# Moving operands of the feed-forwards and of retention's sums at other bytes of a 256-byte line, each group at its own

## The chip, the cores and the metric

The kernel runs on one core of one Trainium2 chip. The metric is the device time in microseconds (us) of one execution; lower is better. Engines are named as in the profile: PE is TensorE's matmul side and PEld its weight load, DVE is VectorE, ACT is ScalarE, POOL is GpSimd, SP is SyncE, which issues most transfers.

## What is computed

Two layers over 512 latent tokens and 256 context tokens of width 1024. Layer 0 is windowed attention, layer 1 is bidirectional retention; each is followed by a SwiGLU feed-forward of width 2816, with the stream modulated ahead of each part. Cut to what matters here:

```python
def swiglu(h, w_in, w_out):
    gate, up = jnp.split(h @ w_in, 2, axis=-1)
    return (jax.nn.silu(gate) * up) @ w_out

def reference(x, c, ctx, c_ctx, ...):
    for i in range(DEPTH):
        ...
        h_x = modulate(rms_norm(x, norm1_g[i]), mx[0], mx[1])
        out_c, out_x = windowed_gqa_sink(...) if i == 0 else bidir_retention(...)
        x = x + mx[2] * out_x
        x = x + mx[5] * swiglu(modulate(rms_norm(x, norm2_g[i]), mx[3], mx[4]), ffn_w_in[i], ffn_w_out[i])
        if need_ctx_out:      # layer 0 alone: the context stream goes the same way
            ...
    return x

def bidir_retention(h_x, h_c, w_qkvg, ...):
    q_x, k_x, v_x, g_x = jnp.split(h_x @ w_qkvg, [qk, 2 * qk, 2 * qk + RET_VWIDTH], axis=-1)
    ...
```

## The kernel before

Activations lie transposed, 128 features on the partitions and tokens along the row, as eight tiles (k = 0 to 7) for 1024 features. Each fp32 value is kept as two parts, a high one (the value rounded to fp32r) and a low one (the rest), and each product is three matmuls: high weights x high activations, low x high, high x low (`mm3`, lines 148 to 150; `product`, line 994; `product_q`, 1413; `product_v`, 1426). ACT rounds (a cast), DVE subtracts (`split`, lines 165 and 166). Weights come as 128x1024 chunks (`wraw`, `wx`), are split into `whi` and `wlo` and used as stationary operand, 128x128 at a time; only `product_v` has the activations as stationary operand and 512 columns of weights moving.

Most large products are done by a seven-product scheme (`seven`): two halves of the inner dimension by two halves of the tokens, seven products instead of eight, with sums of activations (`token_sums`) and of weights (`quarter_sums`) made ahead. The operands are named "11", "12", "22" (the activations themselves) and 1 to 4 (their sums).

- Feed-forward 0 (about 392 to 872 us) has latent and context tokens in one row of 768, cut in two pieces of 384. `A[k, 0]` are tiles of the pool `ep`, tag `aq`; `A[k, 1]` and the sums `S` are tiles of `hq`, also tag `aq` (the helper `quarter`). All are moving operands of `product`. The same tag serves as a weight buffer in the last output group. While it runs, POOL issues 48 transfers of `adaw` (line 271), one behind the other, and DVE turns each into a column of layer 1's modulation (line 274).
- Retention (about 872 to 1368 us) has `h_sum`, the sums of the activations, in pool `hS`, tag `sA`: moving operands of `product_q` with 256 columns, stationary ones of `product_v`.
- Feed-forward 1 (about 1368 to 1716 us) has the activations `hx` (pool `hX`) and their sums `sA` (pool `fp`), 256 columns at a time, and the products' results `ax` (pool `fa`; a high and a low tile each), 512 columns, moving operands of the output products. Weights go round a ring of three pools, `rp`, `hW` and `fp`, two buffers each.

Pools are taken in order from the two ends of a partition, and in a pool the tags lie one behind the other in the order of their first tile. A tile of 512 or 768 fp32 columns is 8 or 12 times 256 bytes, so all tiles of a tag begin at the same byte of a 256-byte line. The helper `off_grid` puts a small tile into a pool (POOL writes zeros to it), by which what follows in the pool begins at another byte. A framework orders each engine's instructions and sets the semaphores from the tiles' uses; the time at which a tile's memory comes free is that of the last use of what lay there.

Of the kernel before, what the change touches and what calls it, by code (L numbers as in the profile page):

```python
# [9 lines left out]
F32R = mybir.dt.float32r  # L10
# [6 lines left out]
KT = D // P  # L17
# [32 lines left out]
def dit_kernel(ctx, tc, xT, cT, crow, small, consts, masks, tabs0, tabs1, jtab, adaQ, adaN, adaT, wst, out):  # L50
    nc = tc.nc
# [10 lines left out]
    def T(pool, cols, tag, bufs, dt=F32):  # L62
        return pool.tile([P, cols], dt, tag=tag, bufs=bufs, name=tag)
# [159 lines left out]
    def t_h(s):  # L223
        return T(hpool[0], 512, ("h", "hc")[s], (16, 8)[s], F32R)

    def off_grid(pool, cols):

        nc.gpsimd.memset(T(pool, cols, "off%d" % cols, 1), 0.0)

    def h_tiles(s):  # L230
        hi = t_h(s)
# [309 lines left out]
    with tc.manual_schedule(engines={mybir.EngineType.PE, mybir.EngineType.DVE, mybir.EngineType.Activation}):  # L541
# [56 lines left out]
        end = ada_unit(UNITS[0], wu[0])  # L598
# [11 lines left out]
        end = ada_unit(UNITS[1], wu[1])  # L610
# [320 lines left out]
    end = lambda: ends.pop(0)()  # L931
# [43 lines left out]
    ep = E.enter_context(tc.tile_pool(name="ep", bufs=1, reuse_waits="tile"))  # L975
# [4 lines left out]
    for s, d in WO_ORDER:  # L980
        out_part(s, d, 0, KT)
        if (s, d) == (1, 4):
            ln_exp_turn()
            scaled = rms(0, bank=pT)[1]
    A.close()

# [24 lines left out]
    hq = Q.enter_context(tc.tile_pool(name="hq", bufs=1, reuse_waits="tile", side="right"))  # L1011
    fp = F.enter_context(tc.tile_pool(name="fp", bufs=1, reuse_waits="tile"))
# [2 lines left out]
    bank = lambda n: T(psF, 512, n, 2)[:, 0:384]  # L1015
    fp32 = [T(ep, 2 * WIDE, "act", 5) for _ in range(4)]
    tm = [fp32[k % 4][:, k // 4 * WIDE:(k // 4 + 1) * WIDE] for k in range(KT)]
    A = {(k, 0): parts(T(ep, 768, "aq", 8, F32R)) for k in range(KT)}
    A.update({(k, 1): parts(quarter()) for k in range(KT)})

    def latent_shape(w):

# [53 lines left out]
    def new_act():  # L1076
        return T(ep, 2 * WIDE, "act", 5, F32R)
# [209 lines left out]
    for gsz in FFN_GROUPS:  # L1287
        acts = []
        for i in range(gsz):
# [4 lines left out]
            else:  # L1294
                a, end = seven(last_sum if f == PLAIN else None)
# [29 lines left out]
    hS = H.enter_context(tc.tile_pool(name="hS", bufs=1, reuse_waits="tile", side="right"))  # L1325
# [2 lines left out]
    qa = R.enter_context(tc.tile_pool(name="qa", bufs=1, reuse_waits="tile"))  # L1328
    qp = R.enter_context(tc.tile_pool(name="qp", bufs=1, reuse_waits="tile"))
    W4 = lambda n: T(psR, 512, n, 2)  # L1330
    h_sum = [(T(hS, 512, "sA", 16, F32R), T(hS, 512, "sA", 16, F32R)) for _ in range(KT)]
    h_first = [T(hpool[0], 512, "aq", 12, F32R) for _ in range(4)]
    h_rest = [(T(hpool[0], 512, "aq", 12, F32R), T(hpool[0], 512, "aq", 12, F32R)) for _ in range(4)]
    chunk_base = wpos[0]
# [160 lines left out]
    for hd in range(RH):  # L1495
# [187 lines left out]
        r, z = mv[:, 8:12], mv[:, 12:16]  # L1683
# [77 lines left out]
        if hd < RH - 1:  # L1761
            for d in range(KT):
# [4 lines left out]
        hM, hW, hX = (ctx.enter_context(tc.tile_pool(name=n, bufs=1, reuse_waits="tile", side="right"))  # L1767
                      for n in ("hM", "hW", "hX"))
        ahead = []

        def first_weights(room, behind=(), low=()):
            raw = w_raw()
            hi, lo = room()
            ahead.append((hi, lo))
            after(nc.scalar.copy(hi, raw), behind)
            after(nc.vector.tensor_tensor(lo, raw, hi, op=sub), low)

        wx_parts = lambda: (T(qw, 1024, "wx", 4, F32R), T(qw, 1024, "wx", 4, F32R))
        hW_parts = lambda: (T(hW, 1024, "whi", 2, F32R), T(hW, 1024, "wlo", 2, F32R))
        hm = [T(hM, 512, "hm", 8) for _ in range(KT)]  # L1780
        off_grid(hX, 16)
        hx = [(T(hX, 512, "hx", 16, F32R), T(hX, 512, "hx", 16, F32R)) for _ in range(KT)]
        off_grid(hX, 48)
        done = []

        def second_norm(k, c, behind=()):
# [17 lines left out]
                    after(ins, done[d - 4:d - 3])  # L1804
        done += [second_norm(k, HALVES[1]) for k in (KT - 2, KT - 1)]
        for i in (6, 7):
            first_weights(hW_parts, done[5:6], done[i:i + 1])

    scaled = []

# [10 lines left out]
    fa = F.enter_context(tc.tile_pool(name="fa", bufs=1, reuse_waits="tile"))  # L1821
    fp = F.enter_context(tc.tile_pool(name="fp", bufs=1, reuse_waits="tile"))
    ring += [rp, rp, hW, hW, fp, fp]
    wsel[0] = 4
    sh2 = T(fp, 16, "sh2", 1)
    sA = [(T(fp, 512, "sA", 16, F32R), T(fp, 512, "sA", 16, F32R)) for _ in range(KT)]
    off_grid(fp, 48)
    operand_a = operands(lambda k, half: [a[:, HALVES[half]] for a in hx[k]], sA)

    def new_act():  # L1830
        return T(fa, 512, "ax", 10, F32R), T(fa, 512, "ax", 10, F32R)

    def half(i):
        return [(a[:, HALVES[i]], b[:, HALVES[i]]) for a, b in hx]
# [245 lines left out]
```

## Time and profile before

| | |
|---|---|
| median of 3 runs | 1717.99 us (1717.43 to 1718.41) |
| profiled execution, first to last instruction | 1716.5 us (the profile has no other time of it) |
| PE busy | 1701.4 us, 11094 matmuls |
| DVE, ACT, POOL busy | 1337.5, 839.8, 124.2 us |
| granted TensorE clock | 1.000 |

The first number in a row of the order of time is the start in us from the span's start, the second the time until the last of its matmuls ended. A matmul's own time holds its way through the array, which overlaps the next one's; how fast PE goes is read from start to start. An `xN` joins N matmuls of the same names that follow each other. PE busy is therefore near 100% wherever it does not wait.

### The profile page before, as it was taken

The page shows a single profiled execution, that of the slowest core. Times are in us where ns is not written, and L with a number is a line of the kernel's source. Part 1 is how long each engine was busy: PE and PEld are TensorE (multiplying, and loading weights), DVE is VectorE, ACT ScalarE, POOL GpSimd, SP SyncE. Part 2 cuts the span into 40 slices and gives each one's busy share as a digit, 9 for nine tenths or more (in the row PEclk, how much of TensorE's full clock was granted, in tenths as well). Part 3 has the DMA queues.
Part 4 walks back from the last instruction along what each step waited for, and adds up shares of the span by engine and source line. Part 5 has one row for each costly group of instructions (what it writes and reads, how often), then busy time and mean ns, then how long its engine had stood idle before and what let it go on. Part 6 is the DMA issues. An engine that isn't in the chain of part 4 may idle for free.

```text
span 1716.5 us, 28196 instructions
## 1 busy us (share of the span) xinstructions
PE 1701.4 (99%) x11094; PEld 1535.9 (89%) x11094; DVE 1337.5 (78%) x2425; ACT 839.8 (49%) x1509; POOL 124.2 (7%) x266
## 2 busy tenths in 40 slices
PE   8999999999999999999999999999999999999999
PEld 5888878899999999999998898898898999999997
DVE  6897786488878787878799858758768998878774
ACT  5677786264424243343565624525434655445442
POOL 0033443000000000000000000000000100000000
PEclk9999999999999999999999999999999999999999
DMA  9500014233344434343434534433433333233322
GB/s 377 228 27 26 14 52 172 74 124 111 99 134 136 135 118 152 123 141 115 137 100 135 187 102 133 160 99 125 159 99 110 99 99 123 77 121 107 103 74 86
DMA packets 61908, 205.67 MB, mean 120 GB/s; under 512 B 6864, under 2 KB 7760, under 8 KB 61648
## 3 DMA queue, kind: packets, MB, share of 16 engines
q1 hardware_dynamic: 54864, 178.71, 31.2%
q0 software_dynamic: 6912, 25.17, 4.9%
q8 instruction: 87, 1.43, 0.3%
q14 instruction: 45, 0.37, 0.1%
HBM read 201.75 MB, written 2.10 MB: 119 GB/s over the span
## 4 chain that ended last, share of the span: by engine, by line
PE 87%; DVE 7%; DMA 3%; ACT 1%; issue 1%; POOL 0%; SPq 0%; DVEq 0%; ACTq 0%; POOLq 0%
PE Y L994 15%; PE Z L994 7%; PE pj L148 7%; PE pj L150 7%; PE pj L149 7%; PE Z L1426 6%; PE X L994 4%; PE Y L1413 3%; PE pO L809 2%; PE pT L784 2%; PE S L764 2%; PE pj L1426 2%; PE X L1413 2%; PE X L150 1%; PE Y L149 1%; PE Y L148 1%
## 5 line engine op out<-in xcount | busy, mean ns | idle before, releaser
L994 PE MATMUL Y<-aq,whi 128*128 128x384 f32 x640 | 173.4, 335 | 0.0
L254 DVE SCALAR_TENSOR_TENSOR res<-pj,mod,res 128x512 f32<-128x512 f32 (+1 forms) x102 | 74.3, 729 | 57.9 <-PE pj L150 57.3
L994 PEld LDWEIGHTS Y<-aq,whi 128*128 128x128 f32 x640 | 116.6, 188 | 0.7 <-DVE aq L1063 0.3
L140 ACT CAST whi<-wraw 128x1024 fp32r<-128x1024 f32 x75 | 78.4, 1050 | 68.0 <-PE Z L150 27.5
L141 DVE TENSOR_TENSOR wlo<-wraw,whi 128x1024 fp32r<-128x1024 f32 x75 | 91.2, 1222 | 20.4 <-ACT whi L140 19.7
L994 PE MATMUL Y<-aq,wlo 128*128 128x384 f32 x320 | 106.9, 334 | 0.0
L274 DVE CUSTOM_DVE_ANT_0 y<-adaw,crow,small_sb 128x1024 bf16<-128x1024 f32 x64 | 81.8, 1278 | 20.7 <-DMA adaw<-in_adaT_dram 20.7
L1343 ACT CAST whi<-wraw 128x1024 fp32r<-128x1024 f32 x55 | 57.4, 1050 | 69.9 <-PE Y L150 52.6
L1426 PE MATMUL Z<-whi,sA 128*128 128x512 f32 x256 | 80.4, 390 | 0.0
L1344 DVE TENSOR_TENSOR wlo<-wraw,whi 128x1024 fp32r<-128x1024 f32 x55 | 66.7, 1220 | 16.4 <-ACT whi L1343 16.3
L101 ACT ACTIVATE pr<-pr,stat,qs 128x513 f32<-128x513 f32 (+2 forms) x96 | 74.1, 775 | 10.0 <-DVE stat L771 7.2
L778 POOL TENSOR_SCALAR pr<-pr,stat 128x512 f32<-128x512 f32 (+2 forms) x96 | 67.3, 707 | 72.1 <-DVE stat L777 51.6
L148 PE MATMUL pj<-ax,whi 128*128 128x512 f32 x176 | 68.9, 392 | 0.0
L150 PE MATMUL pj<-ax,whi 128*128 128x512 f32 x176 | 68.7, 390 | 0.0
L149 PE MATMUL pj<-ax,wlo 128*128 128x512 f32 x176 | 68.5, 389 | 0.0
L271 POOL DMA_DIRECT2D adaw<-in_adaT_dram x48 | 25.6, 533 | 511.2 <-DVE mod L274 412.3
L148 PE MATMUL pj<-act,whi 128*128 128x512 f32 (+1 forms) x156 | 60.2, 386 | 0.5 <-DVE res L254 0.5
L994 PEld LDWEIGHTS Y<-aq,wlo 128*128 128x128 f32 x320 | 60.1, 188 | 0.0
L994 PE MATMUL Y<-sA,whi 128*128 128x256 f32 x304 | 60.0, 280 | 0.0
L149 PE MATMUL pj<-act,wlo 128*128 128x512 f32 (+1 forms) x156 | 60.0, 384 | 0.0
L150 PE MATMUL pj<-act,whi 128*128 128x512 f32 (+1 forms) x156 | 59.5, 382 | 0.0
L765 DVE CUSTOM_DVE_ANT_0 pr<-S,mask,qs 128x256 f32<-128x256 f32 (+1 forms) x96 | 52.8, 563 | 8.1 <-PE S L764 6.2
(626 smaller groups left out, 5574.8 us busy)
## 6 DMA issues: line engine op xcount, KB each, us to landing
wraw<-in_wst_dram SPq DMA_DIRECT2D x231, 512.0 KB, 3.7
adaw<-in_adaT_dram POOLq DMA_DIRECT2D x48, 512.0 KB, 3.9
wx<-in_wst_dram SPq DMA_DIRECT2D x28, 512.0 KB, 4.4
adan<-in_adaQ_dram SPq DMA_DIRECT2D x16, 512.0 KB, 6.7
adan<-in_adaN_dram SPq DMA_DIRECT2D x16, 512.0 KB, 8.3
res<-in_xT_dram SPq DMA_DIRECT2D x16, 256.0 KB, 5.1
q<-in_adaN_dram SPq DMA_DIRECT2D x16, 256.0 KB, 5.0
aq<-in_adaN_dram SPq DMA_DIRECT2D x12, 256.0 KB, 5.5
```

Of the source, the lines that this page charges most:

```text
L101: ins = nc.scalar.activation(*args, **kw)
L140: after(nc.scalar.copy(hi, raw), behind)
L141: after(nc.vector.tensor_tensor(lo, raw, hi, op=sub), low)
L148: after(nc.tensor.matmul(o, whi, xhi, start=first, stop=False), behind)
L149: nc.tensor.matmul(o, wlo, xhi, start=False, stop=False)
L150: return nc.tensor.matmul(o, whi, xlo, start=False, stop=last)
L254: return nc.vector.scalar_tensor_tensor(res[d], o, mods[l, s][:, part, d:d + 1], res[d], mult, add)
L274: tiled.append(nc.vector.tensor_tensor_reduce(junk, w, cr[:, s * 1024:(s + 1) * 1024], 1.0, sm_t[:, C_ADAB + l * 48 + j:C_ADAB + l * 48 + ...
L778: nc.gpsimd.tensor_scalar(pt[:, :n], pt[:, :n], st[:, 6 + e:7 + e], 1.0, op0=mult, op1=mult)
L994: ins = nc.tensor.matmul(o, p, r, start=first and k + i == 0, stop=k == 3 and i == 2, skip_group_check=not first)
L1413: ins = nc.tensor.matmul(o[:, e * SC:(e + 1) * SC], p[:, ws], r, start=first and k + e + i == 0, stop=k == 3 and i == 2, skip_group_check= ...
L1426: ins = nc.tensor.matmul(o, p, r, start=first and k + i == 0, stop=k == 3 and i == 2, skip_group_check=not first)
```

## The change

Pads are put into the pools so that groups of tiles begin at other bytes of a line. Some tags are cut in two for this (`sA` into `sA` and `sB`, `hx` into `hx` and `hy`, `ax` into `ax` and `ay`); the sizes and the number of tiles stay. No matmul is added or removed. In the built programs the operands begin at these bytes of a 256-byte line (modulo 256), with the number of matmuls:

| group | columns | matmuls | before | after |
|---|---|---|---|---|
| feed-forward 0, `A[k, 0]` (pool `ep`) | 384 | 576 | 0 | 128 |
| feed-forward 0, `A[k, 1]` and sums (pool `hq`) | 384 | 1296 | 0 | 32 |
| retention, sums 1 and 4 / 2 and 3, moving | 256 | 192 / 192 | 0 | 32 / 128 |
| retention, the same as stationary operand | 512 | 192 / 192 | 0 | 32 / 128 |
| feed-forward 1, `hx` k = 0 to 3 / 4 to 7 | 256 | 372 / 600 | 64 | 32 / 160 |
| feed-forward 1, sums 1 and 4 / 2 and 3 | 256 | 456 / 456 | 64 | 96 / 224 |
| feed-forward 1, `ax` high / low | 512 | 352 / 176 | 0 | 128 / 64 |
| feed-forward 1, weights in `hW` (a third of the ring) | - | - | 0 | 64 |
| other weights as stationary operand | - | - | 0 | 0 |
| attention's `hc` (not changed) | 256 | 432 | 192 | 192 |

The last output group of feed-forward 0 has some of its weights in `aq` buffers of `ep`, which go to 128 (144 matmuls of 256 columns).

```diff
@@ -223,9 +223,9 @@
     def t_h(s):
         return T(hpool[0], 512, ("h", "hc")[s], (16, 8)[s], F32R)
 
-    def off_grid(pool, cols):
-
-        nc.gpsimd.memset(T(pool, cols, "off%d" % cols, 1), 0.0)
+    def off_grid(pool, cols, tag="off"):
+
+        nc.gpsimd.memset(T(pool, cols, "%s%d" % (tag, cols), 1), 0.0)
 
     def h_tiles(s):
         hi = t_h(s)
@@ -1015,8 +1015,12 @@
     bank = lambda n: T(psF, 512, n, 2)[:, 0:384]
     fp32 = [T(ep, 2 * WIDE, "act", 5) for _ in range(4)]
     tm = [fp32[k % 4][:, k // 4 * WIDE:(k // 4 + 1) * WIDE] for k in range(KT)]
+    off_grid(ep, 32)
     A = {(k, 0): parts(T(ep, 768, "aq", 8, F32R)) for k in range(KT)}
+    off_grid(ep, 32, "end")
+    off_grid(hq, 8)
     A.update({(k, 1): parts(quarter()) for k in range(KT)})
+    off_grid(hq, 56)
 
     def latent_shape(w):
 
@@ -1328,7 +1332,12 @@
     qa = R.enter_context(tc.tile_pool(name="qa", bufs=1, reuse_waits="tile"))
     qp = R.enter_context(tc.tile_pool(name="qp", bufs=1, reuse_waits="tile"))
     W4 = lambda n: T(psR, 512, n, 2)
-    h_sum = [(T(hS, 512, "sA", 16, F32R), T(hS, 512, "sA", 16, F32R)) for _ in range(KT)]
+    off_grid(hS, 8)
+    even = [(T(hS, 512, "sA", 8, F32R), T(hS, 512, "sA", 8, F32R)) for _ in range(4)]
+    off_grid(hS, 24)
+    odd = [(T(hS, 512, "sB", 8, F32R), T(hS, 512, "sB", 8, F32R)) for _ in range(4)]
+    off_grid(hS, 32)
+    h_sum = [t for two in zip(even, odd) for t in two]
     h_first = [T(hpool[0], 512, "aq", 12, F32R) for _ in range(4)]
     h_rest = [(T(hpool[0], 512, "aq", 12, F32R), T(hpool[0], 512, "aq", 12, F32R)) for _ in range(4)]
     chunk_base = wpos[0]
@@ -1777,10 +1786,15 @@
 
         wx_parts = lambda: (T(qw, 1024, "wx", 4, F32R), T(qw, 1024, "wx", 4, F32R))
         hW_parts = lambda: (T(hW, 1024, "whi", 2, F32R), T(hW, 1024, "wlo", 2, F32R))
+        off_grid(hW, 16)
+        hW_first = [hW_parts()]
+        off_grid(hW, 48)
         hm = [T(hM, 512, "hm", 8) for _ in range(KT)]
-        off_grid(hX, 16)
-        hx = [(T(hX, 512, "hx", 16, F32R), T(hX, 512, "hx", 16, F32R)) for _ in range(KT)]
-        off_grid(hX, 48)
+        off_grid(hX, 8)
+        hx = [(T(hX, 512, "hx", 8, F32R), T(hX, 512, "hx", 8, F32R)) for _ in range(4)]
+        off_grid(hX, 32)
+        hx += [(T(hX, 512, "hy", 8, F32R), T(hX, 512, "hy", 8, F32R)) for _ in range(4)]
+        off_grid(hX, 24)
         done = []
 
         def second_norm(k, c, behind=()):
@@ -1804,7 +1818,7 @@
                     after(ins, done[d - 4:d - 3])
         done += [second_norm(k, HALVES[1]) for k in (KT - 2, KT - 1)]
         for i in (6, 7):
-            first_weights(hW_parts, done[5:6], done[i:i + 1])
+            first_weights(lambda: hW_first.pop() if hW_first else hW_parts(), done[5:6], done[i:i + 1])
 
     scaled = []
 
@@ -1823,12 +1837,22 @@
     ring += [rp, rp, hW, hW, fp, fp]
     wsel[0] = 4
     sh2 = T(fp, 16, "sh2", 1)
-    sA = [(T(fp, 512, "sA", 16, F32R), T(fp, 512, "sA", 16, F32R)) for _ in range(KT)]
-    off_grid(fp, 48)
+    off_grid(fp, 8)
+    even = [(T(fp, 512, "sA", 8, F32R), T(fp, 512, "sA", 8, F32R)) for _ in range(4)]
+    off_grid(fp, 32)
+    odd = [(T(fp, 512, "sB", 8, F32R), T(fp, 512, "sB", 8, F32R)) for _ in range(4)]
+    off_grid(fp, 8, "end")
+    sA = [t for two in zip(even, odd) for t in two]
     operand_a = operands(lambda k, half: [a[:, HALVES[half]] for a in hx[k]], sA)
 
+    off_grid(fa, 32)
+    ax_hi = [T(fa, 512, "ax", 5, F32R)]
+    off_grid(fa, 48)
+    ax_lo = [T(fa, 512, "ay", 5, F32R)]
+    off_grid(fa, 48, "end")
+
     def new_act():
-        return T(fa, 512, "ax", 10, F32R), T(fa, 512, "ax", 10, F32R)
+        return [(r.pop() if r else T(fa, 512, n, 5, F32R)) for r, n in ((ax_hi, "ax"), (ax_lo, "ay"))]
 
     def half(i):
         return [(a[:, HALVES[i]], b[:, HALVES[i]]) for a, b in hx]
```

On POOL, ahead of the transfers of `adaw`, where the attention's pools end and feed-forward 0's begin:

```order
 L778 TENSOR_SCALAR pr<-pr,stat 128x512 x4
+L228 MEMSET off_4633 128x32
+L228 MEMSET end_4643 128x32
+L228 MEMSET off_4645 128x8
+L228 MEMSET off_4655 128x56
 L271 DMA adaw<-in_adaT_dram 128x1024 x48
```

Four memsets stand ahead of the 48 transfers on their queue. The pads of retention and of feed-forward 1 stand among POOL's additions for the later norms (`y`).

On DVE, in retention's first head, where the sums' low parts (`sA`, now also `sB`), the sums of weights (`wx`, `wraw`) and the weights' low parts (`wlo`) are made, before:

```order
L1371 SCALAR_TENSOR_TENSOR qk_9668<-qk_9668,mod10_76,qk_9640 128x256
L1541 TENSOR_TENSOR wraw_10043<-wx_10039,wraw_10043 128x1024
L166 TENSOR_TENSOR sA_9613<-qk_9668,sA_9612 128x512
L1529 TENSOR_TENSOR gate_9929<-gate_9929,X_9927 128x256
L166 TENSOR_TENSOR sA_9615<-qk_9640,sA_9614 128x512
L1529 TENSOR_TENSOR gate_9930<-gate_9930,X_9927 128x256
L1344 TENSOR_TENSOR wlo_10050<-wraw_10043,whi_10049 128x1024
L1549 TENSOR_TENSOR wx_10053<-wx_10041,wraw_10043 128x1024
```

and in the changed program (its lines are nine higher there):

```order
L166 TENSOR_TENSOR sA_9615<-qk_9678,sA_9614 128x512
L166 TENSOR_TENSOR sB_9627<-qk_9654,sB_9626 128x512
L166 TENSOR_TENSOR sA_9617<-qk_9682,sA_9616 128x512
L1464 TENSOR_TENSOR dx_9924<-hn_9926 128x128
L1538 TENSOR_TENSOR gate_9943<-gate_9943,X_9941 128x256
L1538 TENSOR_TENSOR gate_9944<-gate_9944,X_9941 128x256
L1550 TENSOR_TENSOR wraw_10057<-wx_10053,wraw_10057 128x1024
L1558 TENSOR_TENSOR wx_10067<-wx_10055,wraw_10057 128x1024
L1353 TENSOR_TENSOR wlo_10064<-wraw_10057,whi_10063 128x1024
```

All of the sums' low parts are now done ahead of the first sum of weights, and the difference `wx` stands ahead of the first `wlo` instead of behind it.

On ACT, at the start of feed-forward 1, where the sums' casts (`sA`, `sB` from `hm`) stand among casts of the first output weights (`whi`), before:

```order
L107 ACTIVATE hn_14521<-X_14291 128x512
L165 CAST sA_14273<-hm_13891 128x512
L140 CAST whi_14723<-wraw_14721 128x1024
L165 CAST sA_14275<-hm_13887 128x512
L165 CAST ax_14519<-hn_14521 128x512
L165 CAST sA_14277<-hm_13892 128x512
L107 ACTIVATE hn_14528<-X_14293 128x512
```

and in the changed program:

```order
L107 ACTIVATE hn_14551<-X_14323 128x512
L165 CAST sA_14295<-hm_13911 128x512
L165 CAST sB_14307<-hm_13908 128x512
L165 CAST sA_14297<-hm_13912 128x512
L165 CAST ax_14317<-hn_14551 128x512
L165 CAST sB_14309<-hm_13909 128x512
L165 CAST sA_14299<-hm_13913 128x512
L140 CAST whi_14753<-wraw_14751 128x1024
L107 ACTIVATE hn_14558<-X_14325 128x512
```

Three more casts of sums and that of `ax` pass ahead of the second output weight. PE's own order is the same but for one score matmul of retention, which stands six places earlier.

## The prediction

> **What bounds the kernel now.** I read the page first, then the busy time by stretches, then the order of time on the matmul engine (PE) at the first and last matmul of long unbroken runs.
>
> ```profile
> span 1716.5 us, 28196 instructions
> PE 1701.4 (99%) x11094; PEld 1535.9 (89%) x11094; DVE 1337.5 (78%) x2425; ACT 839.8 (49%) x1509; POOL 124.2 (7%) x266
> PEclk9999999999999999999999999999999999999999
> PE 87%; DVE 7%; DMA 3%; ACT 1%; issue 1%; POOL 0%; SPq 0%; DVEq 0%; ACTq 0%; POOLq 0%
> ```
>
> PE is busy 99% of the span at the full granted clock, and 87% of the chain that ended last is PE. By stretches (feed-forward 0, retention, feed-forward 1):
>
> ```profile
> core 0: us, PE busy (x) PEld busy (x) DVE busy (x) ACT busy (x) POOL busy (x), PEclk, DMA share, GB/s
> 450.00:600.00 150.00, 150.00 (x864) 143.10 (x863) 118.05 (x178) 53.31 (x83) 8.97 (x17) 1.00 0.40 130
> 900.00:940.00 40.00, 39.63 (x254) 35.69 (x254) 38.95 (x53) 21.13 (x33) 0.00 (x0) 1.00 0.40 132
> 1400.00:1500.00 100.00, 100.00 (x713) 93.88 (x713) 83.14 (x117) 48.19 (x81) 0.00 (x0) 1.00 0.31 97
> ```
>
> In both feed-forwards PE has no gap, while VectorE (DVE) has 32 us of 150 and 17 us of 100 left. So what counts is the time from one matmul's start to the next one's, and that depends on more than the columns. I take it from the first row of an unbroken run and the first row after it (or its last row), with the number of matmuls between them:
>
> ```profile
> start us, us, engine line op out<-in xcount [idle before <-releaser]
> 300.71 0.28 PE L149 MATMUL S<-hc,rope 128*128 128x256 f32 x1
> 303.21 0.28 PE L150 MATMUL S<-hc,k 128*128 128x256 f32 x1
> 342.94 0.28 PE L148 MATMUL pj<-hc,whi 128*128 128x256 f32 x1
> 345.65 0.28 PE L150 MATMUL pj<-hc,whi 128*128 128x256 f32 x1
> 425.74 0.34 PE L994 MATMUL Y<-aq,whi 128*128 128x384 f32 x1
> 483.99 0.39 PE L148 MATMUL pj<-act,whi 128*128 128x512 f32 x1
> 962.45 0.39 PE L1426 MATMUL Z<-whi,sA 128*128 128x512 f32 x1
> 978.77 0.27 PE L1716 MATMUL X<-const_sb,gate 128*128 128x128 f32 x1
> 1007.75 0.28 PE L1413 MATMUL Y<-aq,whi 128*128 128x256 f32 x1
> 1033.66 0.40 PE L1426 MATMUL X<-whi,aq 128*128 128x512 f32 x1
> 1454.36 0.40 PE L148 MATMUL pj<-ax,whi 128*128 128x512 f32 x1
> 1476.15 0.28 PE L994 MATMUL Y<-hx,whi 128*128 128x256 f32 x1
> 1515.73 0.40 PE L148 MATMUL pj<-ax,whi 128*128 128x512 f32 x1
> ```
>
> - Moving and stationary operand both at byte 0 of a line: 384 columns, (483.99 - 425.74)/336 = 173.4 ns; 512 columns, (978.77 - 962.45)/72 = 226.7 ns, and for ax (1476.15 - 1454.36)/96 = 227.0 ns; 256 columns, (1033.66 - 1007.75)/216 = 120.0 ns.
> - Moving at byte 64, stationary at 0, 256 columns (hx and sA of feed-forward 1): (1515.73 - 1476.15)/336 = 117.8 ns.
> - Moving at byte 192, stationary at 0, 256 columns (hc): two speeds, (303.21 - 300.71)/22 = 113.6 ns and (345.65 - 342.94)/23 = 117.8 ns.
>
> From 256 to 512 columns at byte 0 one column costs (226.7 - 120.0)/256 = 0.417 ns. So what is added to the columns is 120.0 - 106.7 = 13.3 ns at byte 0, the same at all three widths; 11.1 ns in the usual state off it; 6.9 ns in the short state. All the kernel's matmuls of this kind load their weights while the one before streams, so I read the added time as the two readers meeting in the same part of the line, decided by the difference between the moving operand's byte and the weights' byte. That is an inference: the rows show differences of 0, 64 and 192 alone, and none of the new ones (32, 96, 128, 160, 224).
>
> **The change part by part.** Counts are from the loops.
>
> 1. Feed-forward 0: 1680 product matmuls and 192 of the plain products, 384 columns, go from byte 0 to 32 (1296) or 128 (576). They can be no slower than the columns alone (160.0 ns) and have no measured upper end; the nearest rows are 117.8 and 113.6 against 120.0, so 2.2 or 6.4 ns saved each: 4.1 or 12.0 us.
> 2. Output products of feed-forward 1: 528 matmuls of 512 columns on ax go from 0 to 128 (high part) and 64 (low part). One third of the weights (the hW buffers) go to 64 too, so 56 low-part matmuls meet weights at their own byte and save nothing: 472 x 2.2 or 6.4 = 1.0 or 3.0 us.
> 3. Retention's sums: 384 moving ones of 256 columns go from 0 to 32 or 128, and 384 of 512 columns have them as stationary operand, where the difference becomes 224 or 128: 768 x 2.2 or 6.4 = 1.7 or 4.9 us. Also 144 matmuls in the last output group of feed-forward 0 find their weights in feed-forward buffers at 128: 0.3 or 0.9 us.
> 4. Feed-forward 1: 288 + 684 matmuls on hx and 912 on sA, 256 columns, are off the line already (117.8 ns) and go from 64 to 32 and 160 (hx, hy), 96 and 224 (sA, sB). Against weights at 0 or 64 the difference is always an odd multiple of 32. Bounds by the nearest rows: 113.6 (4.2 ns saved each, 7.9 us) and 120.0 (2.2 ns lost each, 4.1 us); I take no change as the base, being between the two.
>
> Base sum, with every matmul that leaves byte 0 at the usual off-line price: 4.1 + 1.0 + 1.7 + 0.3 = 7.1 us. Of the two offsets the rows show, one has the short state, in one of its two rows; so I let a quarter of the 3256 moved from byte 0 and of the 1884 of point 4 fall into it: 0.25 x 5140 x 4.2 ns = 5.4 us more.
>
> 5. The writers. The casts that fill ax and sA take the same time at byte 0 and at 64, so moving them costs nothing:
>
> ```profile
> L166 DVE TENSOR_TENSOR sA<-qk,sA x8: 679/681/683, 894.9 to 903.4; 128x512 fp32r<-128x512 f32 x8
> 1392.33 0.69 DVE L166 TENSOR_TENSOR sA<-hm,sA 128x512 fp32r<-128x512 f32 x1
> ```
>
> 6. Fifteen more memsets of 8 to 56 columns on GpSimd (POOL). Four stand ahead of the first of the 48 transfers of adaw and wait for PE and DVE to leave the attention's memory.
>
> ```profile
> 389.45 0.75 POOL L271 DMA_DIRECT2D adaw<-in_adaT_dram  x1 [91.08 <-PE pj L311]
> 441.63 1.28 DVE L274 CUSTOM_DVE_ANT_0 y<-adaw,crow,small_sb 128x1024 bf16<-128x1024 f32 x1
> ```
>
> POOL idles 91 us ahead of that issue, for PE itself, and its data is first read 52 us later: a memset cannot eat that cover unless it holds POOL past about 430 us. The eleven others stand among POOL's additions for the later norms, or behind them; I count them as 0, and if one of them waited for a late transfer, PE would wait for the norm behind it (a few us at most, in the range).
>
> 7. Moved instructions. Before retention's first sum product DVE now does the difference of two weights (wx, 1.2 us) ahead of the low part wlo that this product needs.
>
> ```profile
> 904.38 1.22 DVE L1344 TENSOR_TENSOR wlo<-wraw,whi 128x1024 fp32r<-128x1024 f32 x1
> 905.52 1.21 DVE L1549 TENSOR_TENSOR wx<-wx,wraw 128x1024 f32<-128x1024 f32 x1
> 906.17 0.28 PE L1413 MATMUL Y<-sA,whi 128*128 128x256 f32 x1
> 906.29 0.28 PE L1413 MATMUL Y<-sA,wlo 128*128 128x256 f32 x1
> ```
>
> wlo ended at 905.6, PE reads it at 906.29, so 0.7 us are spare and about 1.1 are taken; DVE is busy 38.95 of 40 us here and cannot catch up at once. I take 0.5 us of wait, bounds 0 and 2. In feed-forward 1 casts of the sums (0.6 us each) pass ahead of an output weight that PE reads only behind the 96 matmuls of the third plain product, 11 us at 117.8 ns; 0.
>
> Sum: -7.1 - 5.4 + 0.5 = -12.0 us. The sum is against the profiled span of 1716.5 us; the median of the runs, 1717.99 us, is 1.5 us above it and I subtract from the median: 1706 us. If PE gets 12 us shorter DVE has still some 30 us of each 150 spare in feed-forward 0, so nothing else is the bound there.
>
> The Trainium skill's page "TensorE: Matmul & The Clock Gate", section "Back-to-back issue gap", puts the gap at the columns over 2.4 GHz plus about 2.5 ns: with 10.8 ns saved on each of the 3256 and 8.6 on each of the 1884 the sum would be 51 us by that figure, an estimate. No row here comes below 6.9 ns added, so I do not use it.
>
> **The rivals.**
>
> A. All moved groups fall into the short state: 3256 x 6.4 + 1884 x 4.2 = 28.8 us less, so 1690 us. For it: hc at 192 does run at 113.6 over whole stretches, and the new offsets spread over the line. Against: hx and sA at 64 show 117.8 alone, in runs of 336.
>
> B. No change that counts, 1716 to 1719 us: offsets that are multiples of 32 gain little for 384 and 512 columns (where no row off the line exists), and feed-forward 1 goes back to 120.0, 4.1 us lost against the 4.1 us of point 1, with the wait of point 7 on top of what is left. The Trainium skill's same page, section "Step-by-step: what each phase is for", says that PE reads the moving operand and the weights through two independent ports, so that a weight load takes nothing from a running matmul. By that rule no byte would matter and this rival would be the result; the rows disagree for 256 columns (120.0, 117.8 and 113.6 ns).
>
> C. Slower: a start at an odd multiple of 32 bytes costs a read more, since every offset that the rows show is a multiple of 64. 1296 + 192 + 1884 = 3372 moving operands stand at such bytes. With x ns each against now, and 2.2 ns gained on the other 1568 or so (3.4 us), it is slower from x of 1.0 ns; at 4.2 ns, the step between the two states, it is 14.2 - 3.4 = 10.8 us more: 1729 us.
>
> **How the numbers follow.** My forecast (gain between 3.5 and 20 us) has 0.56, A 0.16, B 0.17, C 0.11. The time predicted is 1706. The forecast's own range is 1698 to 1714.5; A gives 1690 with 28.8 us as its centre, B reaches 1719, C begins there. Leaving out half of A and most of C, 8 in 10 lie in 1689 to 1721. A change under 0.2% (3.4 us) can hardly be told from none here. Faster by more: 0.54 + 0.16 + 0.05 = 0.75; within it: 0.02 + 0.10 + 0.02 = 0.14; slower: 0.02 + 0.09 = 0.11.
>
> **What would show it.** Right: products of feed-forward 0 at 168 to 171 ns from start to start, in runs of one value; ax at 221 to 225; retention's sums at 114 to 118; the low part of ax on hW weights still at 227; no new idle time of PE over 1 us near 906. Wrong: 173.4 unchanged (B), hx or sA at 120 or more (B or C), 176 and above at byte 32 (C), or a gap on PE behind a memset. The prediction's weakest step is the value at offsets never seen here, and that of the state which a run locks into.

## The result: 0.7% slower, and the profile after

The changed kernel takes 1730.31 us (median, 1728.31 to 1731.23) against 1717.72 us for the kernel before on the same chip (1717.43 to 1718.41): ratio 1.0069, 95% interval 1.0055 to 1.0084, that is 12.6 us slower where 12 us less had been forecast. The profiled execution took 1731.23 us, its span is 13.0 us longer than that of before. From the page, the lines that answer to those of before:

```profile
span 1729.5 us, 28222 instructions
PE 1711.7 (99%) x11094; PEld 1541.6 (89%) x11094; DVE 1340.2 (77%) x2425; ACT 839.7 (49%) x1509; POOL 125.6 (7%) x281
```

DVE and ACT have the same work as before; PE, with the same 11094 matmuls, is busy 10.3 us longer. The same stretches show where (the columns are those of the stretches shown before):

```profile
450.00:600.00 150.00, 150.00 (x859) 143.43 (x858) 116.21 (x176) 54.15 (x85) 8.97 (x17) 1.00 0.40 130
1400.00:1500.00 100.00, 97.96 (x674) 90.83 (x673) 80.69 (x113) 46.27 (x77) 0.00 (x0) 0.98 0.31 95
```

In feed-forward 0 PE still has no gap, but does 859 matmuls in 150 us instead of 864. In feed-forward 1 it does 674 instead of 713 in 100 us, has 2 us of gap, and the clock is not 1.00 all the time. The first and last matmuls of unbroken runs, in the order of time on PE:

```profile
426.78 0.34 PE L994 MATMUL Y<-aq,whi 128*128 128x384 f32 x1
431.01 0.34 PE L994 MATMUL Y<-aq,whi 128*128 128x384 f32 x1
441.43 0.51 PE L994 MATMUL Y<-aq,whi 128*128 128x384 f32 x2
460.65 0.34 PE L994 MATMUL Y<-aq,whi 128*128 128x384 f32 x1
470.88 0.52 PE L994 MATMUL Y<-aq,whi 128*128 128x384 f32 x2
1023.72 0.28 PE L1422 MATMUL Y<-sB,whi 128*128 128x256 f32 x1
1026.57 0.28 PE L1422 MATMUL Y<-sA,whi 128*128 128x256 f32 x1
1029.38 0.28 PE L1422 MATMUL Y<-sB,whi 128*128 128x256 f32 x1
1336.72 0.39 PE L1435 MATMUL Z<-whi,sA 128*128 128x512 f32 x1
1344.88 0.39 PE L1435 MATMUL Z<-whi,sA 128*128 128x512 f32 x1
1588.28 0.40 PE L148 MATMUL pj<-ax,whi 128*128 128x512 f32 x1
1610.58 0.28 PE L994 MATMUL Y<-hx,whi 128*128 128x256 f32 x1
```

- 384 columns at byte 128: 24 matmuls in 4.23 us, 176.3 ns. At byte 32: 59 from 431.01 to 441.43, 176.6 ns, and 59 from 460.65 to 470.88, 173.4 ns. Before: 173.4.
- 256 columns, retention's sums: at byte 128 (`sB`) 24 in 2.85 us, 118.8 ns; at byte 32 (`sA`) 24 in 2.81 us, 117.1 ns. Before: 120.0.
- 512 columns with those sums as stationary operand: 35 in 8.16 us, 233.1 ns. Before: 226.7.
- 512 columns, `ax` (moving at 128, 128, 64): 96 in 22.30 us, 232.3 ns. Before: 227.0.

Over whole groups, from the starts in the two traces (a matmul with more than 40 ns beyond its columns counts as a wait and is left out):

| group | matmuls | mean ns before | mean ns after | us |
|---|---|---|---|---|
| feed-forward 0, 384 columns | 1872 | 173.4 | 175.4 | +3.7 |
| `ax`, 512 columns | 528 | 227.3 | 232.5 | +2.7 |
| sums as stationary operand, 512 columns | 384 | 227.2 | 232.9 | +2.2 |
| retention's sums moving, 256 columns | 384 | 120.0 | 117.7 | -0.9 |
| feed-forward 1, 256 columns | 1884 | 117.8 | 118.5 | +1.3 |

That is 9.0 us; the remaining 4 us are waits and a spell at half clock. What PE waited for (total us, times, longest us), the larger rows from retention on that before does not have, or in the first case has with 0.5 us in all:

```profile
PE pj L148 <- DVE res L254: 3.2, 4, 2.0
PE X L150 <- DVE hy L244: 0.7, 2, 0.5
PE Y L1422 <- DVE wlo L1353: 0.5, 1, 0.5
```

The longest one costs more than its 2.0 us. The stretches around it:

```profile
1412.00:1414.00 2.00, 0.00 (x1) 0.00 (x1) 2.00 (x5) 1.29 (x2) 0.00 (x0) 1.00 0.00 0
1414.00:1416.00 2.00, 2.00 (x8) 1.70 (x9) 1.95 (x4) 1.18 (x2) 0.00 (x0) 0.83 0.00 0
1416.00:1418.00 2.00, 2.00 (x7) 1.61 (x6) 1.74 (x2) 1.17 (x2) 0.00 (x0) 0.50 0.03 8
1418.00:1420.00 2.00, 2.00 (x8) 1.60 (x8) 1.16 (x2) 0.00 (x0) 0.00 (x0) 0.82 0.61 160
```

Behind the gap the granted clock is 0.50 for a while: 2 us lose 0.17, 0.50 and 0.18 of their clock, 1.7 us in all. The Trainium skill's page "TensorE: Matmul & The Clock Gate", section "What's actually happening", says that the array's clock goes to half behind an idle window of some 3.4 us, the windows running freely. The half clock agrees with that; the length does not, as the gap here was only 2.04 us.

### The profile page after: what moved, and what is told of

It is laid out like the page before. It is cut to its first block, busy times and chain, and to the rows that moved or that the text cites. A ratio compares the mean times of both kernels' runs of the same rounds, so it can differ in the third digit from the quotient of the medians.

```text
span 1729.5 us, 28222 instructions
## 1 busy us (share of the span) xinstructions
PE 1711.7 (99%) x11094; PEld 1541.6 (89%) x11094; DVE 1340.2 (77%) x2425; ACT 839.7 (49%) x1509; POOL 125.6 (7%) x281
## 4 chain that ended last, share of the span: by engine, by line
PE 88%; DVE 7%; DMA 2%; ACT 1%; issue 1%; POOL 0%; SPq 0%; DVEq 0%; ACTq 0%; POOLq 0%
PE Y L994 16%; PE Z L994 8%; PE Z L1435 7%; PE pj L148 7%; PE pj L150 7%; PE pj L149 7%; PE X L994 4%; PE Y L1422 3%; PE pO L809 2%; PE S L764 2%; PE pT L784 2%; PE pj L1435 2%; PE X L1422 1%; PE Z L150 1%; PE Z L149 1%; PE Z L148 1%
## 5 line engine op out<-in xcount | busy, mean ns | idle before, releaser
L994 PEld LDWEIGHTS Y<-aq,whi 128*128 128x128 f32 x640 | 117.1, 188 | 0.6 <-ACT sq L1175 0.3
L140 ACT CAST whi<-wraw 128x1024 fp32r<-128x1024 f32 x75 | 78.3, 1049 | 66.9 <-PE Z L150 27.5
L141 DVE TENSOR_TENSOR wlo<-wraw,whi 128x1024 fp32r<-128x1024 f32 x75 | 91.4, 1223 | 20.3 <-ACT whi L140 19.9
L1352 ACT CAST whi<-wraw 128x1024 fp32r<-128x1024 f32 x55 | 57.5, 1050 | 70.8 <-PE Y L150 52.6
L148 PE MATMUL pj<-ax,whi 128*128 128x512 f32 x176 | 70.0, 398 | 2.0 <-DVE res L254 2.0
L150 PE MATMUL pj<-ay,whi 128*128 128x512 f32 x176 | 70.4, 400 | 0.0
L994 PE MATMUL Y<-sB,whi 128*128 128x256 f32 x304 | 60.2, 281 | 0.0
L1899 ACT CAST whi<-wraw 128x1024 fp32r<-128x1024 f32 x38 | 39.6, 1052 | 39.2 <-DVE wraw L1004 24.4
```

The lines of the kernel that those rows point to most:

```text
L148: after(nc.tensor.matmul(o, whi, xhi, start=first, stop=False), behind)
L150: return nc.tensor.matmul(o, whi, xlo, start=False, stop=last)
L994: ins = nc.tensor.matmul(o, p, r, start=first and k + i == 0, stop=k == 3 and i == 2, skip_group_check=not first)
```

## The experiments

Theory W, formed from the two traces: the time added to a matmul's columns depends on the difference between the two bytes, but its sign depends on the width. At 256 columns the equal byte is nearly the dearest, at 384 and 512 nearly the cheapest. Beside it stands rival O: order and memsets cost, not the bytes. The experiments that stay within the kernel keep PE's matmuls and their number; the fourth, seventh and eighth are programs of matmuls alone.

### 1. The changed order with the bytes of before

The pads move behind the tiles that they shifted, in every pool; two of the places:

```diff
-    off_grid(ep, 32)
     A = {(k, 0): parts(T(ep, 768, "aq", 8, F32R)) for k in range(KT)}
+    off_grid(ep, 32)
     off_grid(ep, 32, "end")
...
-    off_grid(hS, 8)
     even = [(T(hS, 512, "sA", 8, F32R), T(hS, 512, "sA", 8, F32R)) for _ in range(4)]
-    off_grid(hS, 24)
     odd = [(T(hS, 512, "sB", 8, F32R), T(hS, 512, "sB", 8, F32R)) for _ in range(4)]
+    off_grid(hS, 8)
+    off_grid(hS, 24)
     off_grid(hS, 32)
```

> The changed kernel with every pad moved behind the tiles that it shifts: each engine has the changed kernel's instructions in the changed kernel's order, memsets of POOL included, while all operands begin at the bytes of before. It parts the 12.6 us into bytes and order. Theory W (the bytes themselves are dearer: 384 and 512 columns cost 2.6 to 8 ns more per matmul off the weights' byte, as the trace after shows) expects about 1722 us: of the 12.6 us only some 4 to 5 us of waits stay (PE idle near 1376.8 and 1414 as in the changed kernel), and 173.4 and 227 ns from start to start are back. Rival O (the split tags, the moved casts and the memsets on POOL are what costs) expects 1728 to 1731 us.

Measured: 1722.29 us against 1718.06 (ratio 1.0025, 1.0015 to 1.0034). PE, DVE and ACT do the same instructions in the same order as in the changed kernel, and POOL has all its memsets. So some 8 of the 12.6 us are the bytes' and 4.2 the order's and the memsets' (with the half clock behind the gap, which is 1.7 us here too); both theories have a part, W the larger one. The waits stayed: 0.5 us for `wlo` near 906, and in feed-forward 1

```profile
PE pj L148 <- DVE res L254: 1.9, 1, 1.9
PE X L150 <- DVE hy L244: 0.4, 2, 0.2
```

### 2. The pads without their memsets

```diff
-        nc.gpsimd.memset(T(pool, cols, "%s%d" % (tag, cols), 1), 0.0)
+        T(pool, cols, "%s%d" % (tag, cols), 1)
```

In the changed kernel POOL's order of time shows the hold; the additions L211 are the sum of squares of feed-forward 1's norm:

```profile
1369.78 0.12 POOL L228 MEMSET off<- 128x16 f32 x1
1372.48 0.33 POOL L228 MEMSET off<- 128x48 f32 x5 [2.58 <-PE Y L149]
1373.32 0.12 POOL L228 MEMSET off<- 128x32 f32 x1 [0.51 <-PE Y L150]
1373.59 3.59 POOL L211 TENSOR_TENSOR y<-y,sq 128x256 f32<-128x256 f32 x4
```

> The changed kernel with the pads kept as memory, but without the writes of zeros to any pad; order and bytes of all else are the changed kernel's. In the changed kernel the last four additions of POOL for the first norm of feed-forward 1 stand behind eight memsets, of which two wait 2.58 and 0.51 us for PE. If that holds the norm and through it the start of feed-forward 1, the additions end some 4 us earlier, PE's idle time near 1376.8 and 1414 goes, and the time is 3 to 5 us less than the changed kernel's: 1725 to 1727 us. If those idle times come from the casts that stand in another order, it stays at 1729 to 1731 us. All products keep their time from start to start.

Measured: 1728.07 us (ratio 1.0057, 1.0042 to 1.0072; the changed kernel had 1.0055 to 1.0084). PE's wait for `hy` is gone, but the wait for `res` stays at 1.7 us, this time without a half clock behind it. The gain of 2.2 us is not resolved by the runs: the intervals overlap, and the missing half clock alone would be 1.7 us of it. So the memsets do hold the norm, but the long wait has another cause.

### 3. Only feed-forward 1's 256-column operands at the new bytes

```diff
-    off_grid(ep, 32)
-    off_grid(ep, 32, "end")
-    off_grid(hq, 8)
-    off_grid(hq, 56)
...
-    off_grid(hS, 8)
-    off_grid(hS, 24)
-    off_grid(hS, 32)
...
-        off_grid(hW, 16)
-        off_grid(hW, 48)
...
-    off_grid(fa, 32)
-    off_grid(fa, 48)
-    off_grid(fa, 48, "end")
```

> The changed kernel without the pads of feed-forward 0, of retention's sums, of the buffers hW and of ax: every operand of 384 and 512 columns is back at byte 0 like its weights, and only hx (32, 160) and its sums (96, 224) of feed-forward 1 keep the new bytes. Theory W (off the weights' byte 384 and 512 columns lose and 256 gain) expects 173.4 and 227.0 ns back, 9 us less than the changed kernel for them, hx and sums at 116.8 to 119.7 ns: 1717 to 1722 us by how much of the waits stays. Rival O (order and memsets cost) expects no more than the memsets of hW gone, 1726 to 1731 us. Theory C of the prediction (odd multiples of 32 bytes cost) expects hx and its sums to lose here as before: 1722 us or more with 120 ns or more on them.

Measured: 1722.47 us (ratio 1.0027, 1.0016 to 1.0038), as the first experiment. 384 and 512 columns are back at 173.4 and 227.2 ns. In feed-forward 1 the means are 117.1 ns at byte 32, 119.7 at 96, 118.4 at 160, 118.3 at 224: rival C's odd multiples of 32 bytes are not one price. Over the 1884 matmuls that is 118.4 ns against 117.8, so the new bytes of feed-forward 1 gain nothing and cost 1.2 us in this trace. Its time is that of the first experiment all the same: its gap of 2.0 us for `res` has no half clock behind it. So the larger part of the 8 us comes from the wide operands, as the table by groups says (8.6 us for them, -0.9 for retention's moving sums, +1.3 for feed-forward 1).

### 4. Pairs of bytes by themselves

```python
for n in (256, 384, 512):
    for a, b, s in PAIRS:            # byte of the high part, of the low part, of the weights
        for r in range(2 + (n == 256)):
            o = ...                  # a new bank
            for k in range(8):
                ...                  # high x high, low x high, high x low
```

> A kernel of matmuls alone (it computes none of the reference; its output is zeros and a few sums): one block of memory with the moving operands, one with the weights, rounds of 24 matmuls in the pattern high x high, low x high, high x low, at 15 pairs of bytes (moving, weights) for 256, 384 and 512 columns, all twice in turn; no other engine works beside them. Theory D (the difference between moving byte and weights' byte decides) expects: pairs 64/64 and 128/128 like 0/0 (120.0, 173.4, 226.7 ns); 0/64 like 192/0 and 32/64 like 224/0; at 256 columns all other differences below 120.0 (116.8 at 32, 117.8 at 64, 113.6 or 117.8 at 192), at 384 above 173.4 (176 at 128), at 512 above 226.7 (231 to 235). Rival M (the moving operand's own byte decides) expects 128/128 like 128/0 (118.6, 176.0, 232) and 0/64 like 0/0. Rival S (what costs at 512 columns is the step from one moving byte to another, high at 128 and low at 64) expects 128/0 at 227 and only the mixed pairs at 232 or more.

Rows of the second turn (the output is named for the bytes, m moving and w weights; the time of a matmul is from a row's start to the next row's start, over the number of matmuls). The only other work in these rows is one copy of a column by ACT after each.

```profile
526.29 8.79 PE L76 MATMUL m64b_w64b<-mv,st 128*128 128x256 f32 x72
534.92 8.79 PE L76 MATMUL m128b_w128b<-mv,st 128*128 128x256 f32 x72
543.55 8.68 PE L76 MATMUL m32b_w64b<-mv,st 128*128 128x256 f32 x72
...
694.57 11.06 PE L76 MATMUL m0b_w0b<-mv,st 128*128 128x512 f32 x48
705.47 11.37 PE L76 MATMUL m32b_w0b<-mv,st 128*128 128x512 f32 x48
...
738.88 11.36 PE L76 MATMUL m128b_w0b<-mv,st 128*128 128x512 f32 x48
750.08 11.40 PE L76 MATMUL m160b_w0b<-mv,st 128*128 128x512 f32 x48
...
806.03 11.06 PE L76 MATMUL m64b_w64b<-mv,st 128*128 128x512 f32 x48
816.93 11.08 PE L76 MATMUL m128b_w128b<-mv,st 128*128 128x512 f32 x48
827.85 11.35 PE L76 MATMUL m32b_w64b<-mv,st 128*128 128x512 f32 x48
```

Equal bytes, 256 columns: (534.92 - 526.29)/72 = 119.9 ns at 64/64, 119.9 at 128/128 and at 0/0. 512 columns: 227.1 at 0/0, 227.1 at 64/64, 227.5 at 128/128, but 233.3 at 128/0. All pairs, ns from start to start, mean of both turns (0/0 at 256 columns from the second alone, as the first holds the start of the program):

| moving / weights | 0/0 | 32/0 | 64/0 | 96/0 | 128/0 | 160/0 | 192/0 | 224/0 | 16/0 |
|---|---|---|---|---|---|---|---|---|---|
| 256 columns | 119.9 | 117.9 | 117.8 | 119.9 | 118.7 | 117.3 | 113.6 or 117.8 | 118.3 | 113.4 |
| 384 columns | 173.4 | 173.3 | 173.4 | 176.6 | 176.1 | 173.6 | 174.7 | 173.8 | 175.6 |
| 512 columns | 227.0 | 233.4 | 229.1 | 233.6 | 233.3 | 234.2 | 233.2 | 233.1 | 231.6 |

| moving / weights | 64/64 | 128/128 | 0/64 | 32/64 | 128 and 64/0 | 128 and 64/64 |
|---|---|---|---|---|---|---|
| 256 columns | 119.8 | 119.9 | 117.8 | 118.3 | 116.9 | 118.7 |
| 384 columns | 173.5 | 173.9 | 174.7 | 173.7 | 175.4 | 173.9 |
| 512 columns | 227.1 | 227.5 | 233.5 | 233.0 | 232.3 | 233.0 |

0/64 is 192/0 and 32/64 is 224/0 at all three widths (at 256 columns 0/64 took one of 192/0's two speeds). It is the difference modulo 256 with its sign and not the distance: 64/0 takes 229.1 ns at 512 columns, 0/64 233.5. So in these runs the difference decides (theory D); rival M (the moving operand's own byte) falls, and so does S, since 128/0 alone costs 233.3 and a mixed pair no more. And W holds with no other engine at work but for ACT's copies: no difference is cheaper than equality by more than 0.1 ns at 384 columns, and every other one costs 2.1 to 7.2 ns at 512.

One row does not carry over to the kernel. At 384 columns 32/0 costs nothing here (173.3 ns), while the changed kernel has its runs of byte 32 partly at 176.6 and partly at 173.4 ns (the two runs of 59 shown above). By this table feed-forward 0 would lose 576 x 2.7 ns = 1.6 us, not 3.7. That the bytes are the cause all the same is the first experiment's result (173.4 ns in the same order); that a pair of bytes can have two speeds is taken up in the last experiments.

### 5. The sums under one tag again

The kernel of the first experiment, with this:

```diff
-    even = [(T(fp, 512, "sA", 8, F32R), T(fp, 512, "sA", 8, F32R)) for _ in range(4)]
-    odd = [(T(fp, 512, "sB", 8, F32R), T(fp, 512, "sB", 8, F32R)) for _ in range(4)]
...
-    sA = [t for two in zip(even, odd) for t in two]
+    sA = [(T(fp, 512, "sA", 16, F32R), T(fp, 512, "sA", 16, F32R)) for _ in range(KT)]
```

and the same for `h_sum` in pool `hS`.

> The kernel with the bytes of before and all the changed kernel's pads and memsets (the first experiment), but the sums of retention and of feed-forward 1 are one tag sA each again; hx/hy and ax/ay stay split. DVE's casts of these sums then stand where they stood before. The first experiment took 1722.3 us against 1718.1. Theory T (cutting the sums' tag moved their casts ahead of weights' low parts, and that is what makes PE wait about 2.2 us near 1407 and 0.5 us more near 906) expects those two waits gone: 1718.5 to 1720 us, with only what the memsets hold left. Rival H (the memsets alone hold POOL, the norm and all behind it) expects both waits and 1722 us to stay.

Measured: 1718.38 us (ratio 1.0003, 0.9994 to 1.0012): just under the time that theory T expected. 3.7 of the 4.2 us are gone, and with them the waits for `res` (1.9 us) and for `wlo` (0.5 us), and the half clock. The memsets still hold POOL:

```profile
1365.96 0.28 POOL L228 MEMSET off<- 128x16 f32 x4 [2.28 <-PE Y L149]
```

Theory T holds, H falls: 2.28 us on POOL alone cost nothing that the runs can tell. What the tags did can be read on DVE. Before, the low parts of two output weights (`wlo`, L141) stand at:

```profile
1390.59 1.22 DVE L141 TENSOR_TENSOR wlo<-wraw,whi 128x1024 fp32r<-128x1024 f32 x1
1396.33 1.22 DVE L141 TENSOR_TENSOR wlo<-wraw,whi 128x1024 fp32r<-128x1024 f32 x1
```

and in the changed kernel, with the row of ACT that waits for the next chunk:

```profile
1403.48 1.22 DVE L141 TENSOR_TENSOR wlo<-wraw,whi 128x1024 fp32r<-128x1024 f32 x1
1404.62 0.68 DVE L166 TENSOR_TENSOR ay<-hn,ax 128x512 fp32r<-128x512 f32 x1
1405.22 1.22 DVE L141 TENSOR_TENSOR wlo<-wraw,whi 128x1024 fp32r<-128x1024 f32 x1
1406.35 1.22 DVE L1891 TENSOR_TENSOR wlo<-wraw,whi 128x1024 fp32r<-128x1024 f32 x1
1408.29 0.69 DVE L1001 TENSOR_TENSOR wraw<-wraw 128x512 f32<-128x512 f32 x1 [0.72 <-DMA wraw<-in_wst_dram]
...
1411.39 0.69 DVE L1893 TENSOR_TENSOR hm<-wraw,hm 128x512 fp32r<-128x512 f32 x1 [1.16 <-ACT hm L1892]
```

```profile
1408.28 0.62 ACT L1892 CAST hm<-wraw 128x512 fp32r<-128x512 f32 x1 [4.30 <-DMA wraw<-in_wst_dram]
```

The whole changed kernel is 5.6 us late here (PE's first matmul on `ax` starts at 1409.00, before at 1403.36). Counted back from that matmul, the two `wlo` stood 12.8 and 7.0 us ahead of it before, and 5.5 and 3.8 us in the changed kernel, where all eight low parts of the sums stand ahead of both. The raw chunks under the weights are let go late, the next chunk's transfer is late, ACT waits for it (4.30 us), and DVE waits for it and then for ACT (1.16 us), ahead of the additions to `res` that free the banks into which PE writes its sums.

### 6. Feed-forward 1 at byte 16

```diff
-        off_grid(hX, 16)
-        hx = [(T(hX, 512, "hx", 16, F32R), T(hX, 512, "hx", 16, F32R)) for _ in range(KT)]
-        off_grid(hX, 48)
+        hx = [(t[:, 4:516], t[:, 516:1028]) for t in (T(hX, 1088, "hx", 8, F32R) for _ in range(KT))]
...
-    sA = [(T(fp, 512, "sA", 16, F32R), T(fp, 512, "sA", 16, F32R)) for _ in range(KT)]
     off_grid(fp, 48)
+    sA = [(t[:, 4:516], t[:, 516:1028]) for t in (T(fp, 1088, "sA", 8, F32R) for _ in range(KT))]
```

> The kernel of before with hx and its sums (1884 matmuls of 256 columns in feed-forward 1) at byte 16 instead of 64, as pairs of high and low part in one tile; no other operand moves. In the kernel of matmuls alone, 16 bytes off the weights gave 113.4 ns from start to start in all six rounds, 64 bytes 117.8, 0 bytes 119.9. If that holds in the kernel, 1884 x 4.4 ns = 8.3 us go: 1709.5 to 1711 us, unless the pair tiles, which move a few casts of sums on ACT and DVE, bring back one of the waits seen (then up to 1713). If the 113.4 ns is only found where no other engine uses the memory, it stays near 117.8 ns and 1718 us.

Measured: 1719.31 us against 1717.87 (ratio 1.0010, 1.0001 to 1.0019): the gain is missed. Feed-forward 1's matmuls took 118.1 ns in the mean, in runs of 118.7 ns and a few of 113.3, not 113.4. One run of 336 that has both, its first row and the first row behind it:

```profile
1475.86 0.28 PE L994 MATMUL Y<-hx,whi 128*128 128x256 f32 x1
1515.73 0.39 PE L148 MATMUL pj<-ax,whi 128*128 128x512 f32 x1
```

(1515.73 - 1475.86)/336 = 118.7 ns.

### 7. Finer bytes by themselves

The fourth experiment's program with other bytes, weights at 0.

> Again matmuls alone (none of the reference), weights at byte 0 and the moving operand at 0, 4, 8, 16, 24, 40, 48, 80, 112, 144, 176, 208, 240, 248, 252. It asks whether the byte counts within 32 bytes. If the memory is read in pieces of 32 bytes or more, 4 to 24 behave like 0 or like 32 (120.0 or 117.8 ns at 256 columns; 226.7 or 233.4 at 512); but 16 gave 113.4, 175.6 and 231.6, so I expect pieces of 16 bytes or less: 8 and 4 then differ from 0 too. For 384 and 512 columns no byte should be below the equal byte (173.3, 226.7).

Measured at 256 columns: 123.1 ns at 4, 126.6 and 116.8 (first and second turn) at 8, 116.7 and 113.3 at 16, 120.0 at 24 and 40, 118.3 at 48, 120.0 at 80, 114.2 at 112, 118.6 to 119.3 at 144, 176 and 208, 117.2 at 240, 120.0 at 248, 116.7 at 252. At 384 columns 173.3 to 179.7, at 512 from 229.6 (252) to 237.8 (4) against 227.7 at 0. Even 4 bytes count, and at 256 columns one byte can have two speeds (8 and 16 here). None of these is below equality at 512, and at 384 columns the best gains 0.1 ns.

### 8. Does a run stay where it begins?

```python
for turn in range(4):
    for b in BYTES:
        for n, rounds in ((512, 1), (256, 4)):   # 24 matmuls at byte 0, then 96 at byte b
```

> Matmuls alone (none of the reference): runs of 96 matmuls of 256 columns with the moving operand at 15 bytes against weights at 0, each begun four times behind 24 matmuls of 512 columns. The experiment before found 16 bytes at 113.3 ns in the matmuls alone, at 116.7 or 113.3 ns when these were run again, and at 118.7 ns in most of feed-forward 1. It asks whether a byte has one time or several in which a run can lock. If the byte alone decides (theory D as it stood), each byte has one value in all four runs; if the byte sets only which values are possible and the start of a run picks one (theory L), 16, 64 and 192 differ between runs that begin the same way or settle within a run. 112 came to 113.3 ns from 115.9 in both runs before, so L expects it to settle at 113.3 in all four.

Measured: 118.7 ns at 16 and 117.8 at 192 in all four runs, 113.3 at 112 in all four, each time from 116.5 in the first 12; 12, 60 and 220 gave 116.7, 28 gave 115.6, 64 gave 117.8, 20 gave 122.2, the others 117.8 to 121.7. The four runs of a byte, begun alike, agree within 0.1 ns. So 16, 64 and 192 did not differ between runs begun alike, as L had expected as one way to show itself; only 112 settled within its runs. For L speak the experiments together: 16 has three speeds (113.3, 116.7, 118.7) and 192 two, so the byte alone does not decide; it limits which speeds there are. The matmuls right ahead do not pick one: in the fourth experiment 192 stood behind 160 in both turns (113.6 and 117.8 ns), in the seventh 8 behind 4 (126.6 and 116.8). Nor does the output's bank by itself: the eighth goes round its four banks so that every turn begins on another, and nothing changed. What picks one stays open. Of the bytes seen with several starts, 112 alone came to 113.3 each time.

### 9. Feed-forward 1 at byte 112

The sixth experiment with `t[:, 28:540], t[:, 540:1052]`, same order of all instructions.

> The kernel with hx and its sums as pairs in one tile, at byte 112 instead of 16 (all instructions and their order are those of the experiment with 16, which took 1719.3 us at 118.1 ns). If 112 settles at 113.3 ns here as it did in the matmuls alone, 1884 x 4.8 ns = 9.0 us go: 1709 to 1711 us. If the traffic of the other engines keeps it from settling, it stays at 117 to 119 ns and 1717 to 1720 us; I give the two about the same chance.

Measured: 1714.19 us (1712.50 to 1715.24) against 1717.87 us: ratio 0.9979, 0.9970 to 0.9988. That is between the two times expected, and neither. It is the fastest version here, and beats the changed kernel too (0.9979 against 1.0069 of before, some 15 us). One run of 336, its first row and the first row behind it:

```profile
1535.12 0.28 PE L994 MATMUL Y<-hx,whi 128*128 128x256 f32 x1
1573.55 0.39 PE L148 MATMUL pj<-ax,whi 128*128 128x512 f32 x1
```

What PE waited for in feed-forward 1, where before has no wait in the list (two more rows of 0.2 us each are left out):

```profile
PE pj L148 <- DVE res L254: 0.8, 1, 0.8
PE pj L148 <- ACT ax L165: 0.6, 1, 0.6
```

(1573.55 - 1535.12)/336 = 114.4 ns with its small waits, against 117.8 before; without waits the mean is 113.8. So 1884 x 4.0 = 7.5 us of the 9.0 were there, but the time fell by 3.7 only: PE, faster, now waits for DVE and ACT in places where it did not before. Added up over feed-forward 1, what the gaps on PE hold beyond the usual step (matmuls with more than 40 ns beyond their columns) is 1.6 us before and 5.8 us here, 4.2 more. The sixth experiment parts the two possible causes: it has the same order, moved casts and all, at 118.1 ns, and its gaps hold 2.3 us. So 0.6 us came with the pair tiles, and 3.6 us only with the speed (one trace each).

## Why the prediction was wrong, point by point

- **What bounds the kernel**: right. PE's time from start to start carried 9 of the 13 us, with the same matmuls.
- **That the difference of the two bytes decides**: right in so far as 64/64 and 128/128 are 0/0; but a difference can have more than one speed. The step built on it was wrong.
- **Points 1, 2 and 3, the failed step**: the gain seen at 256 columns (2.2 ns, or 6.4) was carried over to 384 and 512 columns as "the nearest rows", next to the finding that the added time at equal bytes was the same 13.3 ns at all widths. That sameness says nothing of the unequal bytes, and no row off the line existed at these widths. Point 1 was -4.1 us and measured +3.7; point 2 -1.0 and +2.7; point 3 -1.7 and +1.3 (-0.9 for the moving sums, +2.2 as stationary operand). That the upper end was open for 384 columns was written down ("no measured upper end"), but the range of the sum did not take it in. (The floor beside it, "no slower than the columns alone", has to read no faster.)
- **The short state for a quarter of 5140**: -5.4 us, and nothing of it came. The state exists, but of the multiples of 32 bytes only 192 showed it in any run here.
- **Point 4**: 0 forecast, +1.3 us measured, inside its bounds. Byte 96 against weights at 0 gave 119.7 ns, nearly equality's price.
- **Point 7, `wlo` at 906**: 0.5 us forecast, 0.5 measured. **The casts of feed-forward 1** were counted as 0, and this failed: the cover named was the time until PE reads that weight, but the late weight held its raw chunk, so a transfer, so DVE, so the bank that PE wanted. That is most of the 4.2 us, the half clock behind the gap included (the fifth experiment took 3.7 us back).
- **Point 6**: memsets 0. Near enough: the norm was held as the sentence in point 6 feared, by PE though and not by a transfer; 0.7 us of wait in the changed kernel, and 0.2 in the fifth experiment.
- **Rivals**: C had the time (1729) by luck: of its 3372 matmuls at odd multiples of 32 bytes, the 1884 of feed-forward 1 cost 0.7 ns each and not 4.2, and retention's at byte 32 gained (117.1 against 120.0). Its sign, 176 ns and above at byte 32, came in part of feed-forward 0 alone; and 128/0, no odd multiple of 32, loses at 384 and 512. A's short state (1690; by its own terms 1689) came to none of the moved groups. By rule B no byte would matter; here it matters at every width (113.3 to 126.7 ns at 256 columns, 173.3 to 179.7 at 384, 227 to 238 at 512), and it is the difference to the weights' byte that counts. The Trainium skill's page "TensorE: Matmul & The Clock Gate", section "Step-by-step: what each phase is for", states two independent read ports, so that a weight load takes nothing from a running matmul; for these matmuls the measurement decides against it. In what way the two reads meet, no run here shows.

## What to carry to other kernels

A price measured at one operand width is no bound for another: before moving operands, time the pair (byte, width) in a loop of matmuls that runs by itself, several times with different starts, since one byte may have several speeds. Keep 384- and 512-column fp32r operands at their weights' byte (no other byte tried gained more than 0.1 ns); for 256 columns look for a byte that settles low each time (here 112), not one that did so once. And when a tile tag is cut in two for its address, compare the order of instructions on the engine that fills it, and follow a late write through the buffer that it holds.

## What the runs showed of the hardware that was not expected

- Many runs of fp32r matmuls settle at values some 3.3 ns apart: 113.3, 116.7, 120.0, 123.3, 126.7 ns at 256 columns, 173.3, 176.7, 180.0 at 384, 226.7 and 233.3 at 512. Others repeat a short pattern with a mean between them (byte 196: 118, 120, 118, 124 ns, mean 120.0). In the eighth experiment the means over twelve matmuls, from the thirteenth on, stayed within 0.4 ns of each other at every byte but 100 (0.6 ns).
- Differences of 4 and 8 bytes count as well: 123.1 ns at 4 and up to 126.7 at 8, slower than the 120.0 at equal bytes.
- A gap of 2.04 us on PE was followed by a clock of 0.50 in the changed kernel, and one of 1.9 us in the first experiment too; gaps of 1.7 and 2.0 us in the second and third were not. So the price of such a wait was up to 1.7 us beyond itself, and its length alone does not decide; what else does, no run here shows.
